# A hybrid decoder layer: the order of the state-space batches, and one run of value products for two attention units

## The chip, the cores and the metric

One core of one Trainium2 chip runs the whole layer (1024 tokens, width 1024, batch 1). The metric is the device time of one execution in microseconds.

## The reference, cut to what matters

The input is normed and projected once; half of the channels go through a diagonal complex state-space recurrence (32 groups of 16 channels, 64 states each), half through an attention over a window of 128 tokens with a sink; both are gated, joined by `w_out`, and a gated per-layer embedding follows.

```python
def s5_branch(u, lam_re, lam_im, log_step, b_re, b_im, c_re, c_im, d, w_glu, b_glu):
    lam_bar = jnp.exp(lam * step)
    b_bar = ((lam_bar - 1.0) / lam)[..., None] * b
    bu = jnp.einsum('blgp,gnp->blgn', uf.astype(jnp.complex64), b_bar)
    _, states = lax.associative_scan(combine, (a, bu), axis=1)
    y = jnp.einsum('blgn,gpn->blgp', states, c).real + d * uf
    g = jax.nn.gelu(y)
    return g * jax.nn.sigmoid(g @ w_glu + b_glu)

def swa_branch(q, k, v, sinks):        # 128 queries see the block before and their own
    scores = jnp.einsum('bnqkgd,bnskd->bnkgqs', qb, kb) * scale
    scores = jnp.where(mask, scores + bias, -jnp.inf)
    m = jnp.maximum(jnp.max(scores, axis=-1, keepdims=True), sink)
    e = jnp.exp(scores - m)
    probs = e / (jnp.sum(e, axis=-1, keepdims=True) + jnp.exp(sink - m))
    return jnp.einsum('bnkgqs,bnskd->bnqkgd', probs, vb)

proj = rms_norm(h, pre_norm_g) @ w_in           # u, z_ssm, q, k, v, z_attn
ssm_out  = s5_branch(u, ...) * silu(z_ssm)
attn_out = swa_branch(q, k, v, sinks) * silu(z_attn)
h = h + rms_norm(concat(ssm_out, attn_out) @ w_out, post_norm_g)
h = h + sigmoid(h @ pl_w_gate + pl_b_gate) * (p @ pl_w_proj)
```

## The kernel before

Most products run in two rounded parts of each operand (`split_to` makes a high and a low part, L91): for each slice of 128 of the contracted axis and each half of 512 tokens there are three matmuls, high by high (L122), high weight by low (L124), low weight by high (L126); `product` issues them. Weights come by DMA into `w_st` and are split by ScalarE (high part, L92) and VectorE (low part, L93).

A planner orders the instructions of every engine ahead of the run: it takes them by priority, which is the order of the program, and by its own model of time. `tc.high_priority(offset=AHEAD)` moves what stands in it 20 places forward; `tc.issue_after(i)` puts instructions behind `i` on the queue of `i`'s engine; `tc.manual_schedule(engines=...)` keeps the engine's instructions in the order of the program. Tiles with one tag share the buffers of `BUFS`; a tile waits until the one before it in its buffer is done with. The queues of all engines are fixed before the run; an instruction that waits holds up those behind it on its engine.

**State-space stage.** The 32 groups go in eight batches of four. For a batch, `into_states` loads the inputs `U` and the coefficients `coef` (SyncE queue), builds the input matrix `mt` (VectorE, three products, L530 to L532), transposes it on TensorE into a bank `tab` (L536) and copies it to `m` (ScalarE), multiplies it by `U` into `w` (L541, copied by ScalarE, L543), sends the halves of `w` crosswise into `w2` (`swapped`, DMAs issued by ScalarE, L591 and L592), makes the direct term (`t7`, through DRAM into `tz`) and the output matrix `qt` (three VectorE products). `phases` makes cosines `co` and sines `si` (six VectorE products). `scan` turns `w` by the phases, scans along time (four `tensor_tensor_scan`, L602) into `s` and swaps `s` into `s2` (DMAs on the SyncE queue). `outputs` turns `s` back, multiplies by `tz` and `qt` into a bank (L615, L617), applies the Gelu (L619) and stores `y` to DRAM. All VectorE products of these functions go through `tt`, so their line is L335. The order is `scan(b)`, `phases(b+1)`, `outputs(b)`, `into_states(b+1)`. `w` and `s` share the two buffers of tag `w`; `w2`, `s2` and `y` the two of tag `sw`; `tz`, `qt`, `co`, `si`, `U` and `coef` have two each, `mt` and `m` one. Between the batches stand the projections of v, q and the gates (11 tiles, 48 matmuls each).

**Attention.** Eight blocks of 128 queries, two units each (`half` 0 and 1, four heads each), so 16 units. A unit's steps: `scores` (TensorE, two banks `tab`, L764 and L765), `maxima` (VectorE, L773 and L781), `exponents` (ScalarE, L788), `normalized` (VectorE for half 0, L798, ScalarE for half 1, L796), `transposed` (TensorE into bank `w` or `y`, L803, copied to `p` by ScalarE, L805), `parted` (VectorE, L811), `values` (TensorE, L821, into the same bank: eight instructions, 64 weight columns each, on one half of the array's columns or the other by kv head; four in block 0), `gated` (VectorE, L826). Every other matmul of the stage uses all 128 columns. A unit starts every four ticks, and a step runs its lag later: `values` at 9 ticks, `gated` at 10. ScalarE's part of the attention stands behind the last batch's Gelu.

**Pieces.** Three ticks in four also run one piece of other TensorE work: 16 pieces of the last two SSM gate projections (`SsmGate`, six matmuls each), from piece 16 on the GLU products (`Glu`, L903, four instructions each), then the state-space half of the output product (`OutHalf`, six matmuls each). Pieces up to 9 stand ahead of the first unit. The GLU reads `y_all`, which is loaded from the stored `y`.

Of the kernel before, what the change touches and what calls it, by code (L numbers as in the profile page):

```python
# [20 lines left out]
P = 128  # L21
# [6 lines left out]
PC = 16  # L28
# [25 lines left out]
def layer_kernel(  # L54
# [6 lines left out]
    with ExitStack() as top:  # L61
# [272 lines left out]
        def tt(o, a, b, op):  # L334
            V.tensor_tensor(out=o, in0=a, in1=b, op=op)  # L335
# [144 lines left out]
        def big(name, tag):  # L480
            return t2([P, WID], F32, name, tag)
# [16 lines left out]
        def of_in(L, c):  # L498
            return L[:, c * GB : c * GB + GB, :].unsqueeze(2).broadcast_to([P, GB, PC, CH])
# [4 lines left out]
        def view_in(t):  # L504
            return t.rearrange("p (g q k) -> p g q k", k=CH, q=PC)
# [4 lines left out]
        def ev(t):  # L510
            return t.rearrange("p (g a b) -> p g a b", a=8, b=16)

        def into_states(b):

            c = b["c"]
            gs = slice(c * GB, (c + 1) * GB)
            U = b["U"] = t2([P, GB, NC], F32, "U", "u")
            nc.sync.dma_start(out=U, in_=u_dr[c // 2][(c % 2) * 64 : (c % 2) * 64 + 64].rearrange("(g q) j c -> (q j) g c", q=PC))
            coef = b["coef"] = t2([P, GB, 4, PC], F32, "coef", "coef")
            with tc.issue_after(loaded.ins):  # L520
                nc.sync.dma_start(out=coef, in_=bc[:, gs])

            t1, mt = big("t1", "ta"), big("mt", "mt")
            def per_in(n):
                return coef[:, :, n, :].unsqueeze(3).broadcast_to([P, GB, PC, CH])

            def per_out(n):
                return coef[:, :, n, :].unsqueeze(2).broadcast_to([P, GB, CH, PC])

            tt(view_in(t1), of_in(LB_re_, c), per_in(0), ALU.mult)  # L530
            tt(view_in(mt), of_in(LB_im_, c), per_in(1), ALU.mult)
            tt(mt, t1, mt, ALU.subtract)  # L532
            m = big("m", "m")
            ps = bank("tab")
            for g in range(GB):
                PE.transpose(ps[:, g * P : (g + 1) * P], mt[:, g * P : (g + 1) * P], ident)  # L536
            S.copy(out=m, in_=ps)
            w = b["w"] = big("w", "w")
            ps = bank("w")
            for g in range(GB):  # L540
                PE.matmul(ps[:, g * NC : (g + 1) * NC], lhsT=m[:, g * P : (g + 1) * P], rhs=U[:, g, :],  # L541
                          start=True, stop=True)
            S.copy(out=w, in_=ps)  # L543
            b["w2"] = swapped(w, nc.scalar)
            ps = bank("tab")
            for g in range(GB):
                PE.matmul(ps[:, g * PC : (g + 1) * PC], lhsT=mt[:, g * P : (g + 1) * P],
                          rhs=coef[:, g, 2, :], start=True, stop=True)
            t7 = b["t7"] = t2([P, GB, PC], F32, "t7", "t7")
            tt(t7, last.unsqueeze(1).broadcast_to([P, GB, PC]),  # L550
               ddt[:, gs].unsqueeze(2).broadcast_to([P, GB, PC]), ALU.mult)
            tt(t7, t7, ps[:, 0 : GB * PC].rearrange("p (g q) -> p g q", q=PC), ALU.add)


            n, o = 2 * CH * PC, t7_dr[c].offset
            tz = b["tz"] = big("tz", "tz")
            for g in range(GB):
                nc.sync.dma_start(out=bass.AP(tensor=t7_dr.tensor, offset=o + g * PC * n + n - PC, ap=[[n, PC], [-PC, CH], [1, PC]]), in_=t7[:, g, :])
            for g in range(GB):
                nc.sync.dma_start(out=tz[:, g * P : (g + 1) * P],  # L560
                                  in_=bass.AP(tensor=t7_dr.tensor, offset=o + g * PC * n + CH * PC, ap=[[n, PC], [-PC, CH], [1, P]]))
            a, qt = big("t2", "ta"), big("qt", "qt")
            tt(view_out(a), of_out(L_re, c), per_out(2), ALU.mult)
            tt(view_out(qt), of_out(L_im, c), per_out(3), ALU.mult)
            tt(qt, a, qt, ALU.add)
            b["qt"] = qt

        def phases(b):
            gs = slice(b["c"] * GB, (b["c"] + 1) * GB)
            co, si = b["co"], b["si"] = big("co", "co"), big("si", "si")  # L570

            def a_(t):
                return t[:, gs, :].unsqueeze(3).broadcast_to([P, GB, 8, 16])

            def b_(t):
                return t[:, gs, :].unsqueeze(2).broadcast_to([P, GB, 8, 16])

            a = big("t3", "ta")
            tt(ev(a), a_(e1[1]), b_(e0[1]), ALU.mult)
            tt(ev(co), a_(e1[0]), b_(e0[0]), ALU.mult)  # L580
            tt(co, co, a, ALU.subtract)
            a = big("t4", "ta")
            tt(ev(a), a_(e1[0]), b_(e0[1]), ALU.mult)
            tt(ev(si), a_(e1[1]), b_(e0[0]), ALU.mult)
            tt(si, si, a, ALU.add)

        swaps = []

# [5 lines left out]

        def scan(b):
            w, w2, co, si, c = (b[n] for n in ("w", "w2", "co", "si", "c"))
            tt(w2, w2, si, ALU.mult)
            tt(w, w, co, ALU.mult)
            tt(w, w, w2, ALU.add)
            s = b["s"] = big("s", "w")  # L600
            for g in range(GB):
                V.tensor_tensor_scan(out=s[:, g * NC : (g + 1) * NC],  # L602
                                     data0=r8[:, c * GB + g : c * GB + g + 1].broadcast_to([P, NC]),
                                     data1=w[:, g * NC : (g + 1) * NC], initial=0.0, op0=ALU.mult, op1=ALU.add)
            b["s2"] = swapped(s, nc.sync)

        def outputs(b):
            s, s2, co, si, c, U, tz, qt = (b[n] for n in ("s", "s2", "co", "si", "c", "U", "tz", "qt"))
            tt(s2, s2, si, ALU.mult)
            tt(s, s, co, ALU.mult)  # L610
            tt(s, s, s2, ALU.subtract)
            y = t2([P, GB, NC], F32, "y", "sw")
            ps = bank("y")
            for g in range(GB):
                PE.matmul(ps[:, g * NC : (g + 1) * NC], lhsT=tz[:, g * P : (g + 1) * P], rhs=U[:, g, :],  # L615
                          start=True, stop=False)
                PE.matmul(ps[:, g * NC + 1 : (g + 1) * NC], lhsT=qt[:, g * P : (g + 1) * P],  # L617
                          rhs=s[:, g * NC : (g + 1) * NC - 1], start=False, stop=True)
            b["gelu"] = S.activation(y, ps.rearrange("p (g c) -> p g c", c=NC), AF.Gelu_apprx_tanh)  # L619
            for g in range(GB):  # L620
                r = (c % 2) * 64 + g * PC
                b["stored"] = nc.sync.dma_start(out=y_dr[c // 2][r : r + PC].rearrange("q i c -> i q c"), in_=y[:, g, :])
# [62 lines left out]
        batch = [dict(c=c) for c in range(G // GB)]  # L685
        k_copies = [partial(copy_k, kv, part) for kv in range(2) for part in (kk_hi, kk_lo)]
        with tc.high_priority(offset=AHEAD):
            into_states(batch[0])
            phases(batch[0])
        project_k()  # L690
# [1 line left out]
                 + [partial(project_z_ssm, m) for m in range(2)])  # L692
        for c, b in enumerate(batch):
            with tc.high_priority(offset=AHEAD):
                scan(b)
                if c + 1 < len(batch):
                    phases(batch[c + 1])
                outputs(b)
                if c + 1 < len(batch):
                    into_states(batch[c + 1])  # L700
            for f in tiles[len(tiles) * c // len(batch) : len(tiles) * (c + 1) // len(batch)]:
                f()
                if k_copies and c > 1:
                    with tc.issue_after(w_last[0].ins):
                        k_copies.pop()()
# [260 lines left out]
        def run_pieces(lo, hi):  # L966
            for n in range(lo, hi):
                for f in pieces.get(n, ()):
# [1 line left out]

        units = [Unit(i) for i in range(2 * NB)]

        steps = ((Unit.gated, 10), (Unit.values, 9), (Unit.transposed, 6), (Unit.parted, 6), (Unit.normalized, 5),
                 (Unit.exponents, 3), (Unit.maxima, 1), (Unit.scores, 0))
        n, ahead, end = min(pieces), 10, max(pieces) + 1
        run_pieces(n, ahead)
        n = ahead
        bq = {0: queries(0)}
        for t in range(4 * len(units) + steps[0][1]):
            for step, lag in steps:  # L980
                i, r = divmod(t - lag, 4)
                if r == 0 and 0 <= i < len(units):
                    with tc.high_priority(offset=AHEAD), behind(ssm_end["gelu"]):
                        step(units[i])
            if t % 8 == 3 and t // 8 + 1 < NB:
                bq[t // 8 + 1] = queries(t // 8 + 1)
            if t % 4 != 1:
                run_pieces(n, n + 1)
                n += 1
        run_pieces(n, end)  # L990


        pls = []
# [191 lines left out]
```

## Time and profile before

| | us |
|---|---|
| median of 3 runs | 532.2 (531.94 to 533.16) |
| profiled execution, its own time | 531.67 |
| its span, first to last instruction | 529.9 |
| TensorE matmul busy | 516.9 (98%) |
| TensorE weight load busy | 409.0 (77%) |
| VectorE busy | 374.6 (71%) |
| ScalarE busy | 211.7 (40%) |

A row of a timeline gives the start, the time until the last of its instructions ended, engine, line, operation, names, shapes and count; in brackets the engine's idle time ahead of it and what ended that. A matmul's record is longer than the time after which the next one can end, since matmuls overlap: what one costs is read from end to end. A queue entry has the engine's name with a q behind it.

### The profile page before, as it was taken

The page shows a single profiled execution, that of the slowest core. Times are in us where ns is not written, and L with a number is a line of the kernel's source. Part 1 is how long each engine was busy: PE and PEld are TensorE (multiplying, and loading weights), DVE is VectorE, ACT ScalarE, POOL GpSimd, SP SyncE. Part 2 cuts the span into 40 slices and gives each one's busy share as a digit, 9 for nine tenths or more (in the row PEclk, how much of TensorE's full clock was granted, in tenths as well). Part 3 has the DMA queues.
Part 4 walks back from the last instruction along what each step waited for, and adds up shares of the span by engine and source line. Part 5 has one row for each costly group of instructions (what it writes and reads, how often), then busy time and mean ns, then how long its engine had stood idle before and what let it go on. Part 6 is the DMA issues. An engine that isn't in the chain of part 4 may idle for free.

```text
span 529.9 us, 7312 instructions
## 1 busy us (share of the span) xinstructions
PE 516.9 (98%) x2477; PEld 409.0 (77%) x2477; DVE 374.6 (71%) x865; ACT 211.7 (40%) x442; POOL 27.5 (5%) x69
## 2 busy tenths in 40 slices
PE   7999999999999999997899999999999999999996
PEld 6888888888888888884355766777788788888886
DVE  4879999879789979654878566555756659846232
ACT  5875121311222222124655655566734343333221
POOL 1000000000000000204020211100000000000000
PEclk9999999999999999999799999999999999999999
DMA  7972633445343344547755222101112155125112
GB/s 265 375 239 61 232 86 98 126 109 156 106 127 103 95 137 114 168 140 216 244 176 169 81 71 49 51 21 41 61 58 80 43 176 154 46 81 177 61 40 79
DMA packets 47092, 65.04 MB, mean 123 GB/s; under 512 B 10064, under 2 KB 25936, under 8 KB 47056
## 3 DMA queue, kind: packets, MB, share of 16 engines
q1 hardware_dynamic: 43664, 58.09, 34.5%
q0 software_dynamic: 1536, 4.20, 3.3%
q10 hardware_dynamic: 1856, 2.31, 1.7%
q8 instruction: 19, 0.31, 0.3%
q14 instruction: 17, 0.14, 0.1%
HBM read 44.12 MB, written 11.01 MB: 104 GB/s over the span
## 4 chain that ended last, share of the span: by engine, by line
PE 51%; DMA 2%; DVE 1%; SPq 0%; issue 0%; ACT 0%; ACTq 0%
PE ps_mm L126 9%; PE ps_mm L124 9%; PE ps_mm L122 9%; PE ps_mm L903 5%; PE ps_tab L122 3%; PE ps_tab L124 3%; PE ps_tab L126 3%; PE ps_w L821 2%; PE ps_y L821 2%; PE ps_tab L764 1%; PE ps_tab L765 1%; DMA y_all<-y_dr 1%; PE ps_w L803 1%; PE ps_y L803 1%; DMA y_dr<-y 1%
## 5 line engine op out<-in xcount | busy, mean ns | idle before, releaser
L122 PE MATMUL ps_mm<-x_hi,w_hi 128*128 128x512 f32 x272 | 86.2, 394 | 1.1 <-ACT x_hi L190 1.1
L126 PE MATMUL ps_mm<-x_hi,w_lo 128*128 128x512 f32 x272 | 86.9, 394 | 0.0
L124 PE MATMUL ps_mm<-x_lo,w_hi 128*128 128x512 f32 x272 | 85.7, 393 | 0.7 <-DVE x_lo L191 0.6
L92 ACT ACTIVATE w_hi<-w_st 128x512 fp32r<-128x512 f32 (+1 forms) x63 | 39.1, 621 | 100.9 <-PE ps_mm L124 68.9
L122 PEld LDWEIGHTS ps_mm<-x_hi,w_hi 128*128 128x128 f32 x272 | 50.9, 189 | 11.5 <-ACT x_hi L190 1.5
L124 PEld LDWEIGHTS ps_mm<-x_lo,w_hi 128*128 128x128 f32 x272 | 50.7, 188 | 11.6 <-DVE x_lo L191 1.5
L93 DVE TENSOR_TENSOR w_lo<-w_st,w_hi 128x512 fp32r<-128x512 f32 (+1 forms) x63 | 42.3, 671 | 24.3 <-ACT w_hi L92 24.3
L126 PEld LDWEIGHTS ps_mm<-x_hi,w_lo 128*128 128x128 f32 x272 | 50.7, 188 | 10.0
L903 PE MATMUL ps_mm<-y_all,w_glu 128*128 128x512 f32 x64 | 31.4, 637 | 3.5 <-DMA y_all<-y_dr 3.4
L122 PE MATMUL ps_mm<-h_hi,w_hi 128*128 128x512 f32 (+1 forms) x96 | 30.8, 380 | 0.0
L124 PE MATMUL ps_mm<-h_lo,w_hi 128*128 128x512 f32 (+1 forms) x96 | 30.8, 380 | 0.0
L126 PE MATMUL ps_mm<-h_hi,w_lo 128*128 128x512 f32 (+1 forms) x96 | 30.7, 380 | 0.0
L788 ACT ACTIVATE sc<-sc,mx 128x129 f32<-128x129 f32 x64 | 25.1, 395 | 12.7 <-DVE mx L781 12.5
L903 PEld LDWEIGHTS ps_mm<-y_all,w_glu 128*128 128x128 f32 x64 | 12.3, 203 | 17.7 <-issue 12.5
L1082 DVE SCALAR_TENSOR_TENSOR o_t<-o_t,pls 128x512 f32<-128x512 f32 (+1 forms) x17 | 10.8, 657 | 19.7 <-ACT o_t L1081 19.7
L335 DVE TENSOR_TENSOR sw<-sw,si 128x512 f32<-128x512 f32 x16 | 11.0, 686 | 16.5 <-DMA sw<-s 9.0
L122 PE MATMUL ps_mm<-m_hi,w_hi 128*128 128x512 f32 x64 | 22.1, 405 | 0.0
L126 PE MATMUL ps_mm<-m_hi,w_lo 128*128 128x512 f32 x64 | 21.8, 398 | 0.0
L124 PE MATMUL ps_mm<-m_lo,w_hi 128*128 128x512 f32 x64 | 21.7, 403 | 0.0
L122 PEld LDWEIGHTS ps_mm<-h_hi,w_hi 128*128 128x128 f32 x96 | 18.0, 188 | 3.5
L124 PEld LDWEIGHTS ps_mm<-h_lo,w_hi 128*128 128x128 f32 x96 | 18.1, 188 | 3.5
L126 PEld LDWEIGHTS ps_mm<-h_hi,w_lo 128*128 128x128 f32 x96 | 18.0, 188 | 3.4
(281 smaller groups left out, 1036.7 us busy)
## 6 DMA issues: line engine op xcount, KB each, us to landing
w_st<-in_w_in SPq DMA_DIRECT2D x30, 256.0 KB
w_st<-in_w_out SPq DMA_DIRECT2D x16, 256.0 KB
w_st<-in_w_gate SPq DMA_DIRECT2D x16, 256.0 KB
x<-in_xS SPq DMA_DIRECT2D x8, 512.0 KB
out_T<-o_t SPq DMA_DIRECT2D x15, 256.0 KB
x_sq<-in_xT SPq DMA_DIRECT2D x4, 512.0 KB
x_st<-in_x SPq DMA_DIRECT2D x4, 512.0 KB
x_sq<-in_x SPq DMA_DIRECT2D x4, 512.0 KB
```

What stands on the lines that cost most here:

```text
L92: S.activation(hi, t, AF.Copy)
L93: V.tensor_tensor(out=lo, in0=t, in1=hi.bitcast(F32), op=ALU.subtract)
L122: yield PE.matmul(o, lhsT=wh, rhs=ah(ka, h), start=f, stop=False)
L124: yield PE.matmul(o, lhsT=wh, rhs=al(ka, h), start=False, stop=False)
L126: yield PE.matmul(o, lhsT=wl, rhs=ah(ka, h), start=False, stop=l)
L335: V.tensor_tensor(out=o, in0=a, in1=b, op=op)
L764: PE.matmul(o, lhsT=l, rhs=kk_hi[:, kv, k0 : k0 + wk], start=True, stop=False)
L788: S.activation(self.sc[:, m, :], self.sc[:, m, :], AF.Exp, bias=self.mx[:, m : m + 1], scale=-1.0, accum_out=self.sm[:, m : m + 1])
L803: PE.transpose(pt[:, m * P : (m + 1) * P], self.sc[:, m, 0:P], ident)
L821: PE.matmul(pv[64 * kv : 64 * kv + 64], lhsT=v[:, cols], rhs=p[:, 2 * kv : 2 * kv + 2, :], start=n == 0, stop=n == len(parts) - 1)
L903: PE.matmul(self.ps, lhsT=self.w[:, k, :], rhs=glu_in["y"][:, self.hf, k, :], start=k == 0, stop=k == 3)
L1082: V.scalar_tensor_tensor(out=t, in0=t, scalar=1.0, in1=pls[2 * m + h][:, a : a + n], op0=ALU.add, op1=ALU.mult)
```

## The change

Three parts. The first is the order of the state-space batches: the first half of `into_states` becomes a function `inputs` (loads, `mt`, its transposition, `m`), and the order becomes `inputs(b+1)`, `scan(b)`, `into_states(b+1)`, `phases(b+1)`, `outputs(b)`, with the three VectorE products of `outputs(b)` (two of them explicitly) queued behind the last products of `into_states(b+1)` (`made`) and `phases(b+1)` (`turned`). No buffer is added. The second: `values` runs 12 ticks after the start of a unit of half 0 and 8 after one of half 1, `gated` at 13 and 9, so both units of a block multiply on the same tick. The third: TensorE goes in program order from the first piece to the last.

```diff
-        def into_states(b):
+        def inputs(b):
...
             t1, mt = big("t1", "ta"), big("mt", "mt")
+            b["mt"] = mt
...
             S.copy(out=m, in_=ps)
+
+        def into_states(b):
+
+            c, U, coef, m, mt = (b[n] for n in ("c", "U", "coef", "m", "mt"))
...
-            tt(qt, a, qt, ALU.add)
+            b["made"] = V.tensor_tensor(out=qt, in0=a, in1=qt, op=ALU.add)
...
-            tt(si, si, a, ALU.add)
+            b["turned"] = V.tensor_tensor(out=si, in0=si, in1=a, op=ALU.add)
...
         def scan(b):
             w, w2, co, si, c = (b[n] for n in ("w", "w2", "co", "si", "c"))
+            tt(w, w, co, ALU.mult)
             tt(w2, w2, si, ALU.mult)
-            tt(w, w, co, ALU.mult)
...
-        def outputs(b):
+        def outputs(b, behind):
             s, s2, co, si, c, U, tz, qt = (b[n] for n in ("s", "s2", "co", "si", "c", "U", "tz", "qt"))
-            tt(s2, s2, si, ALU.mult)
-            tt(s, s, co, ALU.mult)
+
+            with ExitStack() as after:
+                for i in behind:
+                    after.enter_context(tc.issue_after(i.ins))
+                tt(s, s, co, ALU.mult)
+                tt(s2, s2, si, ALU.mult)
             tt(s, s, s2, ALU.subtract)
...
         for c, b in enumerate(batch):
             with tc.high_priority(offset=AHEAD):
+                following = batch[c + 1] if c + 1 < len(batch) else None
+                if following:
+                    inputs(following)
                 scan(b)
-                if c + 1 < len(batch):
-                    phases(batch[c + 1])
-                outputs(b)
-                if c + 1 < len(batch):
-                    into_states(batch[c + 1])
+                if following:
+                    into_states(following)
+                    phases(following)
+                outputs(b, [following["made"], following["turned"]] if following else [])
...
-        steps = ((Unit.gated, 10), (Unit.values, 9), (Unit.transposed, 6), (Unit.parted, 6), (Unit.normalized, 5),
-                 (Unit.exponents, 3), (Unit.maxima, 1), (Unit.scores, 0))
+        steps = ((Unit.gated, 13, 9), (Unit.values, 12, 8), (Unit.transposed, 6, 6), (Unit.parted, 6, 6), (Unit.normalized, 5, 5),
+                 (Unit.exponents, 3, 3), (Unit.maxima, 1, 1), (Unit.scores, 0, 0))
...
+        with tc.manual_schedule(engines={mybir.EngineType.PE}):
+            run_pieces(n, ahead)
+            n = ahead
+            bq = {0: queries(0)}
+            for t in range(4 * len(units) + steps[0][2]):
+                for step, half, i in [(s, h, (t - lags[h]) // 4) for s, *lags in steps for h in range(2) if (t - lags[h]) % 4 == 0]:
+                    if 0 <= i < len(units) and i % 2 == half:
+                        with tc.high_priority(offset=AHEAD), behind(ssm_end["gelu"]):
+                            step(units[i])
+                if t % 8 == 3 and t // 8 + 1 < NB:
+                    bq[t // 8 + 1] = queries(t // 8 + 1)
+                if t % 4 != 1:
+                    run_pieces(n, n + 1)
+                    n += 1
+            run_pieces(n, end)
```

## Rows read from the trace of the kernel before

**Rows 1.** The profile page, its first part: busy time, share of the span and instructions of each engine.

```profile
PE 516.9 (98%) x2477; PEld 409.0 (77%) x2477; DVE 374.6 (71%) x865; ACT 211.7 (40%) x442; POOL 27.5 (5%) x69
```

**Rows 2.** Busy time by stretch: the stretch and its length, busy time and instructions of PE, PEld, DVE, ACT and POOL, then TensorE's granted clock (1.00 is 2.4 GHz), share of the DMA engines, GB/s.

```profile
105.00:238.50 133.50, 133.50 (x703) 114.19 (x701) 108.87 (x195) 29.35 (x44) 4.56 (x8) 1.00 0.45 126
238.50:252.00 13.50, 10.15 (x45) 5.98 (x43) 6.36 (x17) 5.86 (x16) 6.17 (x12) 1.00 0.80 216
252.00:259.00 7.00, 5.47 (x10) 2.78 (x11) 4.96 (x17) 3.12 (x6) 0.70 (x1) 0.51 0.86 283
...
271.00:380.00 109.00, 109.00 (x533) 74.45 (x532) 72.00 (x236) 68.73 (x204) 13.14 (x30) 1.00 0.26 74
```

**Rows 3.** Timeline of TensorE where the state-space stage ends: the last matmuls of `SsmGate`, GLU products (L903), the last batch's output products, scores, the first unit's transposes and the first value products (L821).

```profile
238.04 0.62 PE L124 MATMUL ps_mm<-x_lo,w_hi 128*128 128x512 f32 x2
238.50 0.61 PE L126 MATMUL ps_mm<-x_hi,w_lo 128*128 128x512 f32 x2
240.14 1.96 PE L903 MATMUL ps_mm<-y_all,w_glu 128*128 128x512 f32 x4 [1.03 <-DMA y_all<-y_dr]
...
243.49 3.95 PE L903 MATMUL ps_mm<-y_all,w_glu 128*128 128x512 f32 x8
...
250.37 0.38 PE L764 MATMUL ps_tab<-kk,bq 128*128 128x256 f32 x1 [1.33 <-ACT sc L767]
...
253.53 3.78 PE L903 MATMUL ps_mm<-y_all,w_glu 128*128 128x512 f32 x4 [2.42 <-DMA y_all<-y_dr]
257.11 1.06 PE L803 MATMUL ps_w<-ident,sc 128*128 128x128 f32 x4
257.96 4.07 PE L903 MATMUL ps_mm<-y_all,w_glu 128*128 128x512 f32 x8
261.95 0.65 PE L821 MATMUL ps_w<-p,v_f 128*64 128x256 f32 x4
262.54 7.13 PE L903 MATMUL ps_mm<-y_all,w_glu 128*128 128x512 f32 x16
```

**Rows 4.** Timeline of TensorE in the attention: value products of one unit taken in pieces of two instructions between scores, those of another unit in one stretch, and the last stretch of the kernel.

```profile
281.06 0.28 PE L765 MATMUL ps_tab<-kk,bq 128*128 128x256 f32 x1
281.27 0.65 PE L821 MATMUL ps_w<-p,v_f 128*64 128x256 f32 x2
281.85 0.38 PE L764 MATMUL ps_tab<-kk,bq 128*128 128x256 f32 x1
...
304.34 0.61 PE L122 MATMUL ps_mm<-m_hi,w_hi 128*128 128x512 f32 x2
304.88 0.65 PE L821 MATMUL ps_w<-p,v_f 128*64 128x256 f32 x4
305.37 0.60 PE L821 MATMUL ps_w<-p_own,v_step 128*64 128x256 f32 x4
305.90 0.50 PE L124 MATMUL ps_mm<-m_lo,w_hi 128*128 128x512 f32 x1
...
376.10 0.65 PE L821 MATMUL ps_y<-p,v_f 128*64 128x256 f32 x4
```

**Rows 5.** The end of the state-space stage: two of VectorE's waits between 105 and 242 us (in total, times, longest), then rows of ScalarE's and VectorE's timelines.

```profile
DVE sw L335 <- DMA sw<-s: 9.0, 4, 3.1
...
DVE sw L335 <- DMA t_dr<-t: 5.6, 2, 3.0
...
217.31 0.56 ACT L543 COPY w<-ps_w 128x512 f32<-128x512 f32 x1
225.47 0.63 ACT L92 ACTIVATE bq_hi<-q_f 128x512 fp32r<-128x512 f32 x1 [7.60 <-PE ps_y L615]
225.98 0.47 ACTq L591 DMA_DIRECT2D sw<-w  x1
...
244.01 0.58 ACT L619 ACTIVATE y<-ps_y 128x512 f32<-128x512 f32 x1
...
230.81 0.69 DVE L335 TENSOR_TENSOR sw<-sw,si 128x512 f32<-128x512 f32 x1 [1.93 <-DMA sw<-w]
...
234.48 1.37 DVE L602 TENSOR_TENSOR_SCAN s<-r,w 128x128 f32<-128x128 f32 x4
238.96 0.69 DVE L335 TENSOR_TENSOR sw<-sw,si 128x512 f32<-128x512 f32 x1 [3.12 <-DMA sw<-s]
...
253.51 0.87 DVE L798 TENSOR_SCALAR sc<-sc,sm 128x128 f32<-128x128 f32 x4
```

**Rows 6.** Groups of instructions between 265 and 380 us by line, VectorE's and ScalarE's: busy time of the group, mean ns of one, idle time of the engine just before them and what ended it.

```profile
L781 DVE CUSTOM_DVE_ANT_0 sc<-ps_tab,bias,sink 128x128 f32<-128x128 f32 x52 | 15.7, 347 | 0.9 <-DVE ps_tab L773 0.2
L773 DVE COPY_PREDICATED ps_tab<-own,ps_tab 128x256 f32<-128x256 int32 x26 | 11.0, 425 | 6.8 <-PE ps_tab L765 6.5
L93 DVE TENSOR_TENSOR w_lo<-w_st,w_hi 128x512 fp32r<-128x512 f32 x12 | 8.2, 683 | 2.0 <-ACT w_hi L92 2.0
L798 DVE TENSOR_SCALAR sc<-sc,sm 128x128 f32<-128x128 f32 x28 | 6.2, 282 | 0.2
...
L788 ACT ACTIVATE sc<-sc,mx 128x129 f32<-128x129 f32 x52 | 20.4, 395 | 12.7 <-DVE mx L781 12.5
L788 ACT ACTIVATION_READ_ACCUMULATOR sc<-sc,mx 128x1 f32 x52 | 9.8, 189 | 0.0
L796 ACT ACTIVATE sc<-sc,sm 128x128 f32<-128x128 f32 x28 | 9.1, 393 | 1.4 <-DVE sm L793 1.4
```

More of the change, by code (lines that the diff above doesn't have):

```diff
@@ L511, in ev, with per_in, per_out @@
             return t.rearrange("p (g a b) -> p g a b", a=8, b=16)
-        def into_states(b):
+        def per_in(b, n):
+            return b["coef"][:, :, n, :].unsqueeze(3).broadcast_to([P, GB, PC, CH])
+        def per_out(b, n):
+            return b["coef"][:, :, n, :].unsqueeze(2).broadcast_to([P, GB, CH, PC])
+        def inputs(b):
             c = b["c"]
@@ L523, in into_states @@
             t1, mt = big("t1", "ta"), big("mt", "mt")
[L524 to L531, printed above, removed]
+            b["mt"] = mt
+            tt(view_in(t1), of_in(LB_re_, c), per_in(b, 0), ALU.mult)
+            tt(view_in(mt), of_in(LB_im_, c), per_in(b, 1), ALU.mult)
             tt(mt, t1, mt, ALU.subtract)
-            m = big("m", "m")
+            m = b["m"] = big("m", "m")
             ps = bank("tab")
@@ L537, in into_states @@
             S.copy(out=m, in_=ps)
+        def into_states(b):
+            c, U, coef, m, mt = (b[n] for n in ("c", "U", "coef", "m", "mt"))
+            gs = slice(c * GB, (c + 1) * GB)
             w = b["w"] = big("w", "w")
@@ L562, in into_states @@
             a, qt = big("t2", "ta"), big("qt", "qt")
-            tt(view_out(a), of_out(L_re, c), per_out(2), ALU.mult)
-            tt(view_out(qt), of_out(L_im, c), per_out(3), ALU.mult)
-            tt(qt, a, qt, ALU.add)
+            tt(view_out(a), of_out(L_re, c), per_out(b, 2), ALU.mult)
+            tt(view_out(qt), of_out(L_im, c), per_out(b, 3), ALU.mult)
+            b["made"] = V.tensor_tensor(out=qt, in0=a, in1=qt, op=ALU.add)
             b["qt"] = qt
@@ L687, in layer_kernel @@
         with tc.high_priority(offset=AHEAD):
+            inputs(batch[0])
             into_states(batch[0])
@@ L971, in layer_kernel @@
         units = [Unit(i) for i in range(2 * NB)]
-        steps = ((Unit.gated, 10), (Unit.values, 9), (Unit.transposed, 6), (Unit.parted, 6), (Unit.normalized, 5),
-                 (Unit.exponents, 3), (Unit.maxima, 1), (Unit.scores, 0))
+        steps = ((Unit.gated, 13, 9), (Unit.values, 12, 8), (Unit.transposed, 6, 6), (Unit.parted, 6, 6), (Unit.normalized, 5, 5),
+                 (Unit.exponents, 3, 3), (Unit.maxima, 1, 1), (Unit.scores, 0, 0))
         n, ahead, end = min(pieces), 10, max(pieces) + 1
[L976 to L990, printed above, removed]
+        with tc.manual_schedule(engines={mybir.EngineType.PE}):
[13 more added lines that the diff above has]
+            run_pieces(n, end)
         pls = []
```

## Prediction

> **What bounds the kernel now.** The page comes first: TensorE is busy 98% of the span, no other engine over 77% [rows 1]. So only two things can shorten the run: TensorE's few empty or slow stretches, and matmuls that cost more than their columns. The table by stretch shows where to look [rows 2]. From 105 to 238.5 us and from 271 to 380 us TensorE is never empty at the full clock. Between lies one bad place: busy 10.15 of 13.5 us, and then 7 us at a mean granted clock of 0.51, nearly all of it the lower level, 1.2 GHz. The timeline of that place says why [rows 3]: the last gate projection ends at 239.11, the GLU waits for `y_all`, scores wait for ScalarE, the GLU waits again. The slow clock begins after this half-empty stretch. The last batch's Gelu starts only at 244.01 [rows 5]. Here the end of the state-space chain ends last, and TensorE has run out of other work.
>
> The second reading is of the value products inside the full stage [rows 4]. Two 512-column instructions end 0.453 us apart in pairs (238.04 + 0.62 to 238.50 + 0.61, about 0.23 each) [rows 3]; two score instructions about 0.12 each. Around L821 this breaks. The score before ends at 281.34, the two value instructions at 281.92, the next score at 282.23: 0.58, and 0.31 in place of 0.12. So a stretch of L821 costs an entry, and about 0.19 after it on whatever follows. A whole unit in one stretch ends at 305.97 after 304.95: 1.02 for eight, and the next matmul takes 0.43 for 0.23.
>
> **Part one: value products.** From the first stretch [rows 3] to the last [rows 4] the timeline has 31 stretches of L821: 17 of two instructions, 6 of four, one of six, 7 of eight, 120 in all. A stretch of four costs what one of two costs: 262.03 to 262.60 is 0.57 [rows 3]. So the two halves of the columns work side by side, and pieces of two waste that as well. Now: 23 x 0.58 + 1.01 + 7 x 1.02 = 21.5 us, and 31 x 0.19 = 5.9 us behind them, 27.4 us. After: block 0 is one stretch of eight (1.02), seven blocks one of sixteen each. Four more instructions cost 1.02 - 0.58 = 0.44, so sixteen cost 1.02 + 0.88 = 1.90. 7 x 1.90 + 1.02 + 8 x 0.20 = 15.9 us. That is 11.5 us less, on the engine that is never empty there, so all of it counts. It needs both units of a block to be contiguous on TensorE: on one tick the list of steps gives `values` of half 0, then of half 1, and program order lets nothing between.
>
> The Trainium skill (TensorEngine Tiling (Array Packing), Key Properties) says only that a change of tiling mode drains TensorE. By that rule alone the saving would be 23 fewer changes at 0.15 + 0.19, 7.8 us, and the sum below would come to 521.6. The stretches of two and four, which cost the same, speak for the larger number.
>
> **Part two: the end of the state-space stage.** From 239.11 to 262.03 pass 22.9 us. Work done in it at the full rate: 24 GLU instructions at 0.43 (16 in 6.9 us, 262.54 onward, less the 0.2 at its start) 10.3; 16 scores, 16 output products of the last batch and 4 transposes, all taken at the scores' 0.12, 4.3; in all 14.6 us [rows 3, 4]. Lost: 8.3 us, of it some 2 by the clock. With the 11.5 this is the most that the change can give: 531.7 - 11.5 - 8.3 = 511.9 us.
>
> How much comes back depends on when the last Gelu ends (244.6 now) and what TensorE can do meanwhile. Why is it late? `w` of the last batch is copied at 217.87, but its swap is issued at 225.98: it stands on ScalarE's queue behind a `bq_hi` that waits 7.60 us for batch 6's outputs [rows 5]. In the new order `w2` takes the buffer that `scan(6)` frees, not one that `outputs(6)` frees, so the planner can put the swap right behind the copy. That makes the last scan 8 us earlier (Gelu at 236.6). Then VectorE's waits for swaps, 9.0 and 5.6 us [rows 5], 11.5 of it ahead of the last batch. In the new order `into_states(b+1)` and `phases(b+1)` stand between a scan and the use of its swap: nine products of 0.6 us, longer than the swap's 3. I take half of these waits as gained, 6 us, since VectorE also serves the projections, whose work does not move: Gelu at about 230.5. Bounds: 244.6 (nothing gained) and 225 (all of it). The swap's DMAs keep their queues; `U` and `coef` are asked for a batch half earlier on SyncE, behind nothing that waits longer than now. The price: `outputs(b)` comes later on VectorE, and `scan(b+1)` needs `s`'s buffer (tag `w`) back from it; with chain pieces of about 12 us in a batch that takes 20 us now, this is covered.
>
> Program order takes something back here. Now all 16 gate pieces run before the attention; after, pieces 13 to 15 stand behind `scores` of the second unit, which need the banks that ScalarE empties after the Gelu. So TensorE runs dry at 239.1 - 3 x 1.36 = 235.0, and after the Gelu it has 0.9 us of scores and 1.36 us of piece 13 before `transposed` of the first unit. That comes 9.8 us after the Gelu's end (244.59 to 254.38, when the first unit is normalized) [rows 5]. The empty time is Gelu + 9.8 - 237.3, here 3.0 us; 0 at 225, 9.1 at 236.6, 17.1 at 244.6. For the clock I add 0.5 us: a quarter of the 2 that it cost after a longer hole.
>
> **Part three: program order in the attention.** It adds waits: an instruction whose input is late now holds everything behind it, pieces included, which would need no input of the attention. Two distances matter. Between the scores of a half-1 unit and its transposes stand four pieces (5.4), four transposes (0.44) and one set of scores (0.94): 6.8 us; for half 0 also the value run, 8.9 us. The chain that must fit [rows 6]: two L773 0.85, four L781 about 1.2 (started 0.27 apart), four exponents 1.6 + 0.19, and normalizing, on ScalarE 1.6, on VectorE 1.1: 5.4 and 4.9 us, a reciprocal and the handovers not counted. The margin is under 1.4 us for half 1, under 4.0 for half 0. VectorE is busy 72.0 and ScalarE 68.7 of 109 us there [rows 2], so one alien instruction ahead (0.68, L93) fits, two don't. I take 0.25 us for each of eight half-1 units, 2 us. Bounds: 0 (the trace of now has no wait in 109 us), and 3 us for each block, 24 us, if the queues of VectorE and ScalarE put the chain last. `values` of half 1 a tick earlier than now has two pieces (2.7 us) for a copy and a `parted`; that fits. Half 0's longer hold of bank `w` meets `transposed` of the next block only after 0.86 + 0.94 + 1.36 us, in which VectorE must do `gated`, two products of half the columns of L93's 0.68: nothing.
>
> **Sum.** 511.9 + 3.0 + 0.5 + 2.0 = 517.4 us against the profiled execution's own 531.67. The median of the runs lies 0.5 above that one, so the forecast is 517.9 us.
>
> **The rivals.** (a) *The batches end only as early as the freed swap makes them*, the Gelu at 236.6: empty time 9.1 in place of 3.0, and the full 2 us of clock: 511.9 + 9.1 + 2 + 2 + 0.5 = 525.5. Speaks for it: VectorE's queue is 82% busy up to 238.5 [rows 2], so reordering may only move its waits. (b) *The overlap isn't got at all*, since no buffer is added: `s` and `w`, and `w2`, `s2` and `y`, still share two. The Gelu stays at 244.6, and program order, which withholds three pieces, leaves 17.1 us empty: 511.9 + 17.1 + 2 + 2 + 0.5 = 533.5, the gain of part one eaten. Against it: the order of tags lets `w(b+1)` and `w2(b+1)` in right after `scan(b)`. The Trainium skill (Perfetto Trace Analysis, Optimization Strategy) reads gaps that repeat as too few buffers for the next tile; by that rule the waits for `sw` would stay, which is this case. (c) *TensorE waits in the attention*, the one that ends slower: the place is L803 of half 1, the price what its chain exceeds 6.8 us by. Without its 2 us the forecast is 515.9, so from (532.2 - 515.9) / 8 = 2.0 us for each block it decides; at 3 us the time is 539.9. (d) *The value products aren't one run*, because the planner still lets others between: without part one, 529.4.
>
> **Chances.** Forecast 0.62, (a) 0.17, (b) 0.08, (c) 0.10, (d) 0.03. Between 511.5 (511.9 + 0.5, less 0.9 for reading errors) and 527 lie the forecast, (a) and part of (c) with small waits; (b), (d) and the dear half of (c) are left out. A change of 0.2% (1.1 us) is about what a measurement of this kernel can tell from none. Faster: forecast, (a), (d), a third of (b) and 0.03 of (c), 0.88; same: half of (b), 0.04; slower: the rest, 0.08.
>
> **What would show it.** Eight stretches of L821 and some 16 us for them shows part one; more stretches refute it. The last L619 before 235 us, no wait of VectorE for `sw<-s`, and the swap of the last `w` within 1 us of its copy show part two; an L903 or L803 behind an empty TensorE shows how much is left, and a row at clock 0.5 what it cost. Waits of TensorE at L803 after 271 us, twice in each block, would show (c). The prediction is wrong above all if the planner, which orders VectorE and ScalarE by its own model of time, puts `outputs` or the attention's chain late.

## The result and the profile after

The changed kernel takes 522.75 us (522.39 to 523.7) against 532.07 us beside it: a ratio of 0.9826, 95% interval 0.9804 to 0.9849. Forecast were 517.9 us, range 511.5 to 527. The profiled execution's span is 520.7 us, 9.2 us shorter. In what follows runs from different chips are compared by their ratio to the kernel before on the same chip; times "at 532.1" are that ratio times 532.1 us. A hole is a stretch in which TensorE is empty.

TensorE by stretch (columns as in [rows 2]), of the kernel after:

```profile
105.00:230.00 125.00, 125.00 (x661) 106.90 (x660) 107.59 (x198) 30.30 (x46) 6.18 (x14) 1.00 0.50 135
230.00:245.00 15.00, 14.75 (x75) 11.62 (x74) 7.26 (x26) 7.77 (x24) 3.54 (x7) 1.00 0.70 210
245.00:262.00 17.00, 13.79 (x48) 7.14 (x49) 11.18 (x37) 10.79 (x33) 2.44 (x6) 0.90 0.68 212
262.00:370.00 108.00, 104.94 (x536) 75.86 (x535) 72.49 (x230) 66.37 (x195) 10.61 (x25) 0.98 0.26 76
```

The bad place of [rows 2] has shrunk, but the attention, never empty before, now has 3 us empty and a clock below 1.00. The waits of TensorE (in total, times, longest) and the ends of the empty stretches say where:

```profile
PE ps_y L816 <- ACT sc L809: 6.5, 2, 3.5
```

```profile
242.76 0.28 PE L778 MATMUL ps_tab<-kk,bq 128*128 128x256 f32 x1
242.87 1.88 PE L916 MATMUL ps_mm<-y_all,w_glu 128*128 128x512 f32 x4
248.21 1.26 PE L816 MATMUL ps_y<-ident,sc 128*128 128x128 f32 x4 [3.46 <-ACT sc L809]
249.26 4.79 PE L916 MATMUL ps_mm<-y_all,w_glu 128*128 128x512 f32 x8
...
290.35 0.62 PE L126 MATMUL ps_mm<-m_hi,w_lo 128*128 128x512 f32 x2
294.03 1.20 PE L816 MATMUL ps_y<-ident,sc 128*128 128x128 f32 x4 [3.06 <-ACT sc L809]
294.99 0.71 PE L122 MATMUL ps_mm<-m_hi,w_hi 128*128 128x512 f32 x2
295.54 0.62 PE L124 MATMUL ps_mm<-m_lo,w_hi 128*128 128x512 f32 x2
296.00 1.01 PE L126 MATMUL ps_mm<-m_hi,w_lo 128*128 128x512 f32 x2
296.81 1.05 PE L122 MATMUL ps_mm<-m_hi,w_hi 128*128 128x512 f32 x2
297.67 1.05 PE L124 MATMUL ps_mm<-m_lo,w_hi 128*128 128x512 f32 x2
298.52 1.05 PE L126 MATMUL ps_mm<-m_hi,w_lo 128*128 128x512 f32 x2
```

Two holes, both ahead of the transposes (L816 now) of a half-1 unit, whose normalizing (L809) is ScalarE's. What stands behind them is GLU products at the first and output products at the second, which needed nothing of the attention. Behind each hole stands a stretch at the lower clock (columns as in [rows 2]):

```profile
248.25:251.65 3.40, 3.40 (x7) 1.73 (x8) 1.50 (x6) 2.70 (x12) 0.19 (x1) 0.50 0.81 305
294.03:296.03 2.00, 2.00 (x9) 1.36 (x10) 1.13 (x7) 1.40 (x4) 0.19 (x1) 1.00 0.29 99
296.05:299.44 3.39, 3.39 (x9) 2.22 (x7) 0.53 (x1) 0.00 (x0) 0.00 (x0) 0.50 0.05 18
```

Behind the first hole it comes at once. Behind the second it comes after 2 us of work: matmul pairs first end 0.45 us apart, then 0.86 (297.86 to 298.72 and 299.57). At half the clock 3.4 us lose 1.7, so by the rows the holes with their clock cost 3.46 + 3.06 + 1.7 + 1.7 = 9.9 us.

The value products (L834 now), one of the seven long stretches, answer to [rows 4]:

```profile
267.31 1.02 PE L916 MATMUL ps_mm<-y_all,w_glu 128*128 128x512 f32 x2
268.26 0.65 PE L834 MATMUL ps_w<-p,v_f 128*64 128x256 f32 x4
268.74 0.60 PE L834 MATMUL ps_w<-p_own,v_step 128*64 128x256 f32 x4
269.18 0.60 PE L834 MATMUL ps_y<-p,v_f 128*64 128x256 f32 x4
269.61 0.60 PE L834 MATMUL ps_y<-p_own,v_step 128*64 128x256 f32 x4
270.14 0.39 PE L777 MATMUL ps_tab<-kk,bq 128*128 128x256 f32 x1
```

From 268.33 to 270.21, 1.88 us for sixteen, and 0.32 for the next score in place of 0.12. There are eight stretches: 7 x 1.88 + 1.02 + 8 x 0.20 = 15.8 us, against 27.4: 11.6 us less. The whole change is then 532.1 - 8.3 (the loss at the state-space end) - 11.6 + 9.9 = 522.1 us, for 522.75 measured: what the value products gave, the two holes took again but for some 2 us.

The state-space end, ScalarE's timeline at the swap of the last batch, and the Gelu's group (shortest, middle and longest ns, first and last start), against [rows 5]:

```profile
188.46 0.59 ACT L549 COPY w<-ps_w 128x512 f32<-128x512 f32 x1 [2.08 <-PE ps_w L547]
189.07 0.48 ACTq L597 DMA_DIRECT2D sw<-w  x1
```

```profile
L629 ACT ACTIVATE y<-ps_y x8: 581/598/598, 102.9 to 211.9; 128x512 f32<-128x512 f32 x8
```

The swap is issued as its copy ends, and the last Gelu starts at 211.9, not 244.0. Between the start of the first scan and the end of the last Gelu VectorE (the third engine in the row) looks like this, before and then after:

```profile
89.90:244.60 154.70, 153.59 (x811) 130.03 (x809) 125.21 (x225) 35.78 (x55) 6.16 (x13) 1.00 0.46 130
```

```profile
89.90:212.50 122.60, 122.60 (x672) 105.56 (x671) 115.59 (x217) 32.39 (x51) 5.34 (x13) 1.00 0.50 134
```

VectorE's idle time fell from 29.5 to 7.0 us, and 9.6 us of its work, most of it the gates' (`z_half`, `z_tanh`, `w_lo`), now comes after the Gelu: 22.5 + 9.6 = 32.1 us, the whole of the Gelu's shift. The waits for `sw<-s` are not quite gone; the longest that is left is the last batch's, which no batch follows:

```profile
DVE s L335 <- DMA sw<-s: 3.1, 2, 2.6
```

### The profile page after: what moved, and what is told of

Same layout as the page of the kernel before. It is cut to its first block, busy times and chain, and to the rows that moved or that the text cites. A ratio compares the mean times of both kernels' runs of the same rounds, so it can differ in the third digit from the quotient of the medians.

```text
span 520.7 us, 7280 instructions
## 1 busy us (share of the span) xinstructions
PE 506.0 (97%) x2477; PEld 407.7 (78%) x2477; DVE 371.7 (71%) x865; ACT 211.0 (41%) x442; POOL 24.8 (5%) x69
## 4 chain that ended last, share of the span: by engine, by line
PE 92%; DMA 3%; DVE 2%; SPq 1%; ACT 1%; issue 0%; DVEq 0%
PE ps_mm L122 21%; PE ps_mm L126 21%; PE ps_mm L124 21%; PE ps_mm L916 5%; PE ps_tab L122 4%; PE ps_tab L124 4%; PE ps_tab L126 4%; PE ps_w L834 1%; DMA z_th<-z_dr 1%; PE ps_tab L777 1%; PE ps_y L627 1%; PE ps_y L625 1%; PE ps_w L547 1%; PE ps_y L834 1%; PE ps_tab L778 1%; DMA x_st<-in_xT 1%
## 5 line engine op out<-in xcount | busy, mean ns | idle before, releaser
L122 PE MATMUL ps_mm<-x_hi,w_hi 128*128 128x512 f32 x272 | 88.1, 397 | 1.0 <-ACT x_hi L190 1.0
L93 DVE TENSOR_TENSOR w_lo<-w_st,w_hi 128x512 fp32r<-128x512 f32 (+1 forms) x63 | 42.3, 672 | 33.9 <-ACT w_hi L92 30.0
L126 PE MATMUL ps_mm<-m_hi,w_lo 128*128 128x512 f32 x64 | 20.7, 405 | 0.0
L916 PEld LDWEIGHTS ps_mm<-y_all,w_glu 128*128 128x128 f32 x64 | 11.9, 200 | 10.8 <-issue 10.8
L124 PE MATMUL ps_mm<-m_lo,w_hi 128*128 128x512 f32 x64 | 20.3, 399 | 0.0
L1096 ACT ACTIVATE o_t<-ps_mm,hb_gate 128x512 f32<-128x512 f32 (+1 forms) x12 | 7.7, 665 | 24.8 <-PE ps_mm L126 15.9
```

Of the source, the lines that this page charges most:

```text
L93: V.tensor_tensor(out=lo, in0=t, in1=hi.bitcast(F32), op=ALU.subtract)
L122: yield PE.matmul(o, lhsT=wh, rhs=ah(ka, h), start=f, stop=False)
L124: yield PE.matmul(o, lhsT=wh, rhs=al(ka, h), start=False, stop=False)
L126: yield PE.matmul(o, lhsT=wl, rhs=ah(ka, h), start=False, stop=l)
L916: PE.matmul(self.ps, lhsT=self.w[:, k, :], rhs=glu_in["y"][:, self.hf, k, :], start=k == 0, stop=k == 3)
L1096: S.activation(t, o, AF.Tanh, bias=hb_gate[:, m : m + 1], scale=0.5)
```

## The experiments

Each is an edit of the changed kernel unless it says otherwise.

| run | us | ratio, 95% interval | at 532.1 |
|---|---|---|---|
| whole change | 522.75 | 0.9826 (0.9804 to 0.9849) | 522.8 |
| e1 batches alone | 523.89 | 0.9854 (0.9823 to 0.9885) | 524.3 |
| e2 attention alone | 535.2 | 1.0065 (1.0036 to 1.0095) | 535.6 |
| e3 old lags | 517.62 | 0.9737 (0.9700 to 0.9773) | 518.1 |
| e4 no program order | 519.42 | 0.9769 (0.9742 to 0.9795) | 519.8 |
| e5 not behind `made`, `turned` | 522.57 | 0.9799 (0.9735 to 0.9864) | 521.4 |
| e6 values at 13 and 9 | 520.63 | 0.9745 (0.9701 to 0.9788) | 518.5 |
| e7 16 pieces ahead | 519.78 | 0.9723 (0.9678 to 0.9768) | 517.4 |
| e8 e6 and e7 | 514.11 | 0.9629 (0.9586 to 0.9673) | 512.4 |
| e9 no empty pieces | 517.04 | 0.9729 (0.9715 to 0.9742) | 517.7 |
| e10 only `inputs` early | 535.11 | 1.0064 (1.0041 to 1.0088) | 535.5 |
| e11 e8 and e9 | 512.66 | 0.9641 (0.9628 to 0.9654) | 513.0 |

**e1, e2: the two halves apart.** The new batches with the old attention loop, and the old batches with the new one.

> The new order of the state-space batches alone, the attention as before (31 stretches of value products, no program order). First theory (each part pays for itself, and program order in the attention makes two holes of its own): the Gelu of the last batch near 212 us, the loss of 8.3 us at the end of the state-space stage gone, the values as dear as before: 532.1 - 8.3 = about 524 us. Rival (the state-space order is all of the gain, and part one is eaten by program order): the same time as with the whole change, 522.7 us, or less. What tells them apart more is the sum of this run's gain and that of the attention alone.

> The new lags and program order alone, the batches in the old order. First theory: 11.5 us saved on values, and the Gelu stays near 244 us, so that the hole at the end of the state-space stage grows from 8.3 to 17 us or more, as the prediction's rival (b) has it, and the later hole stays: between 530 and 536 us. Rival (program order gives nothing, the batches all): no saving on values to be seen either, 535 us or more with more than eight stretches of values.

The batches alone give 7.8 us: the hole at the end of their stage is gone (TensorE busy 32.00 of 32 us from 230 to 262), and 31 stretches of values remain. The attention alone loses 3.5 us. It has eight stretches, so the saving is there, but TensorE waits 6.0 us for the last batch's outputs, whose Gelu starts at 244.1 us as before:

```profile
PE ps_y L617 <- DVE s L335: 6.0, 1, 6.0
PE ps_y L803 <- ACT sc L796: 3.8, 2, 3.1
PE ps_w L803 <- DVE sc L798: 2.3, 1, 2.3
```

For e2 the first theory holds. For e1 the time doesn't decide: 524.3 us (522.7 to 526.0) is what the first theory expected, and can't be told from the 522.8 of the whole change, which its rival expected. Both are right in part: the batches give 7.8 of the 9.3 us, and the attention's own saving goes into its holes. The two gains alone sum to 7.8 - 3.5 = 4.3 us, not 9.3, so the parts aren't independent: program order with the new lags costs more than it gives unless the Gelu comes early.

**e3, e4: one run of two units, and program order, each taken back.**

```diff
-        steps = ((Unit.gated, 13, 9), (Unit.values, 12, 8),
+        steps = ((Unit.gated, 10, 10), (Unit.values, 9, 9),
```

> The whole change but with values at 9 ticks and gated at 10 for both units, so each unit multiplies values by itself: 16 stretches. First theory: eight stretches more at 0.15 + 0.19 us each, 2.7 us, with the same two holes at the transposes: 525.4 us. Rival (the run of two units itself makes the holes, as it moves what stands between scores and transposes): the holes go and the time is below 521 us.

```diff
-        with tc.manual_schedule(engines={mybir.EngineType.PE}):
+        with ExitStack():
             run_pieces(n, ahead)
```

> The whole change without program order on TensorE in the attention. The planner then makes 22 stretches of values: 5 of two instructions, 4 of four, 2 of six, 11 of eight, 18.4 us and 22 x 0.19 us behind them, 22.5 us against 15.7 us. First theory (the two holes at the transposes and the slow clock behind them, some 11 us, are the price of program order): 522.7 + 6.8 - 11 = 518.5 us. Rival (the holes come from late inputs whatever the order of TensorE): they stay, 529.5 us.

Both are faster than the whole change, by 4.7 and 3.0 us at 532.1. For e3 the rival was right of the second hole: 16 stretches cost more, yet in its place there is only a wait of 0.7 us ahead of values, and the clock stays at 1.00 from 262 us on. The first hole stays, at 2.5 us. The old lags leave two units' values, each by itself, inside the window of a half-1 unit (between its scores and its transposes): they fall one tick and five ticks after the scores. The new ones take all of them out. For e4 the first theory was right: 22 stretches and no wait of TensorE in the attention, 519.8 for 518.5 expected. e4 and e1 differ in the lags alone: 22 stretches for 31 are 4.5 us less, where the prediction's 27.4 us for 31 and the 22.5 above for 22 let 4.9 be expected.

**e6, e7, e8: each hole by its own edit.**

```diff
# e6
+        steps = ((Unit.gated, 14, 10), (Unit.values, 13, 9),
# e7
+        n, ahead, end = min(pieces), 16, max(pieces) + 1
```

> The whole change with the run of values one tick later (13 and 9, gated 14 and 10): still eight stretches, but the run now stands between the scores of a half-1 unit and its transposes, 8.7 us in place of 6.8 us. First theory (the second hole, 3.1 us and the slow clock behind it, comes from the narrow window of half 1, since the run was taken out of it): that hole goes, 522.7 - 5 = 517.5 us. Rival (it comes from the two pieces without TensorE work between GLU and output product): the hole stays, 521 us or more.

> The whole change with all sixteen gate pieces ahead of the attention (16 for 10). First theory (the first hole, 3.5 us, its single transposes and the slow clock, comes from the last gate's z_half, which stands on VectorE ahead of the second unit's maxima and waits for pieces 14 and 15): it goes, 522.7 - 5 = 517.5 us. Rival (the first block's chain with its table load is too long for any order): the hole moves to another of the first transposes, 521 us or more.

> Values at 13 and 9 and all gate pieces ahead: both holes gone by the first theory, 512.5 us, near the floor of 511.9 + 0.5 us that the prediction worked out. By the rivals of the two runs beside it, 519 us or more.

4.3, 5.4 and 10.4 us less than the whole change at 532.1, so the two holes with their clock are worth some 10 us and, within intervals of some 2.5 us each, add up; the first theory was right in all three. In e6 TensorE waits 1.4 us for bank `w` instead, which the later values hold longer. (In all three runs the last block's two units fell apart: nine stretches of values, not eight.) With both edits TensorE's stretches, to be read against the first table of this part:

```profile
230.00:245.00 15.00, 15.00 (x63) 10.77 (x61) 5.81 (x13) 5.62 (x13) 0.64 (x1) 1.00 0.74 248
245.00:262.00 17.00, 17.00 (x65) 8.94 (x66) 15.11 (x52) 12.46 (x42) 6.11 (x11) 1.00 0.68 213
262.00:370.00 108.00, 107.47 (x575) 80.79 (x572) 73.60 (x233) 69.66 (x204) 11.04 (x26) 1.00 0.25 77
```

For the first hole VectorE's and ScalarE's rows of the changed kernel show the way in, and e7, in which the gate's pieces stand ahead, has no first hole:

```profile
241.88 1.09 DVE L879 SCALAR_TENSOR_TENSOR z_half<-ps_mm,preb 128x512 f32<-128x512 f32 x1 [4.96 <-PE ps_mm L126]
242.81 0.32 DVE L794 CUSTOM_DVE_ANT_0 sc<-sc,bias,sink 128x128 f32<-128x128 f32 x1
...
243.18 0.41 ACT L801 ACTIVATE sc<-sc,mx 128x129 f32<-128x129 f32 x1 [3.24 <-DVE mx L794]
244.96 1.06 ACT L886 ACTIVATE z_tanh<-z_half 128x1024 f32<-128x1024 f32 x1
247.14 0.63 ACT L92 ACTIVATE bq_hi<-q_f 128x512 fp32r<-128x512 f32 x1 [1.12 <-DMA bq<-bq_hi]
247.68 1.26 ACT L809 ACTIVATE sc<-sc,sm 128x128 f32<-128x128 f32 x4
...
245.49 0.17 DVE L806 RECIPROCAL sm<-sm 128x4 f32<-128x4 f32 x1
```

The second unit's maxima stand on VectorE behind the last gate's `z_half`, which waits 4.96 us for the pieces that program order put behind the first units. Then its normalizing, whose reciprocal is there at 245.66, stands on ScalarE behind that gate's tanh and a `bq_hi` until 247.68. Which of these instructions alone would make the hole was not tried.

The second hole has a late chain of its own besides the narrow window:

```profile
286.20 0.28 PE L778 MATMUL ps_tab<-kk,bq 128*128 128x256 f32 x1
...
290.92 0.19 ACT L801 ACTIVATION_READ_ACCUMULATOR sc<-sc,mx 128x1 f32 x1
...
293.31 0.17 DVE L806 RECIPROCAL sm<-sm 128x4 f32<-128x4 f32 x1
...
293.59 1.26 ACT L809 ACTIVATE sc<-sc,sm 128x128 f32<-128x128 f32 x4
```

The unit's scores end at 286.48, its sums are there at 291.11, its reciprocal comes only at 293.31, behind the next unit's maxima and products of other work on VectorE, and the transposes start at 294.03. The chain took 7.55 us; the work in its window was done at 290.97, after 4.5 us.

**e9, e11: the empty pieces.** Between GLU and output product two pieces hold no TensorE work.

```diff
-        n += 2
         for m in range(KT):
             OutHalf(m, n)
```

> The whole change (values at 12 and 8) without the two pieces between GLU and output product that hold no TensorE work: the output product's pieces start two earlier. First theory, sharpened by the run with values at 13 (the second hole needs both: the window of half 1, 6.8 us without the values, and two empty pieces in it, which leave 4.1 us): with all pieces full the hole is gone, 517.5 us. Rival (the empty pieces only mark the place, the window is too narrow anyway): the hole moves to another block, 521 us or more.

> Values at 13 and 9, all gate pieces ahead, no empty pieces. First theory: no hole is left to remove, only single transposes that wait for ScalarE's heads one by one, so 513.5 to 514.5 us, the same as without the last edit. Rival (the empty pieces still cost where the first output pieces wait): below 513 us.

e9 removes the second hole too, with the narrow window left as it is; TensorE's one wait at L816 is the first hole's, 3.7 us. So e3 and e6 had not yet told the two conditions apart: the hole needs the narrow window and two empty pieces in it. e11 is no better than e8 (0.9641 in 0.9628 to 0.9654, against 0.9629 in 0.9586 to 0.9673), as the first theory had it, though 513.0 at 532.1 lies under its range and on its rival's bound.

**e5, e10: what moved the Gelu.**

```diff
# e5
-                outputs(b, [following["made"], following["turned"]] if following else [])
+                outputs(b, [])
# e10
+                inputs(following); scan(b); phases(following); outputs(b, []); into_states(following)
```

> The whole change without putting the products of outputs(b) behind made and turned: the order of the functions stays. First theory (VectorE, no longer idle on swaps, is what moved the last Gelu from 244 to 212 us, and the explicit order does that): waits of VectorE for swaps come back in part, the Gelu lands between 220 and 235 us; as TensorE has other work until 235 us the time changes by less than 2 us if the Gelu stays before 228 us, and by up to 8 us beyond. Rival (the order of the functions and the freed buffer do it alone): Gelu at 212 us and 522.7 us.

> The whole change, but of the batches only inputs(b+1) stays early: then scan(b), phases(b+1), outputs(b), into_states(b+1), as before the change. First theory (what moved the last Gelu is that the rest of into_states and phases stand between a scan and the use of its swap, and that w2 gets the buffer that the scan frees): the Gelu falls back to 235 to 244 us, TensorE is empty there as in the run of the attention alone, 530 to 535 us. Rival (loading and transposing the inputs a half batch earlier is what did it): the Gelu stays below 220 us, 522.7 us.

e5 changes nothing: the rival was right, TensorE, VectorE and ScalarE run the same instructions in the same order as with the whole change, and the last Gelu starts at 211.9 again. The 1.4 us between 521.4 and 522.8 are thus what two measurements of one order can differ by, and the lower clock behind the first hole lasts 6.8 us here, not 3.4:

```profile
246.95:253.78 6.83, 6.28 (x11) 2.94 (x12) 3.38 (x9) 3.99 (x15) 0.19 (x1) 0.50 0.69 235
```

e10 puts the last Gelu back to 243.1 and loses the whole gain, so the first theory was right. `phases` stands between a scan and the use of its swap in e10 too, as before the change; what counts is that the rest of `into_states` stands ahead of `outputs`. Without it VectorE waits 11.9 us for `sw<-s`, and the last swap is issued at 224.12, 11.4 us behind its copy. How much of the shift is VectorE's filling and how much the earlier swap was not tried apart.

## Why the prediction was right and where it was not

**Part one, right in count and size.** Eight stretches, 15.8 us for 15.9; e8 at the floor, below, shows that the saving counts in full once the holes are gone. By the rule of the Trainium skill alone (TensorEngine Tiling (Array Packing), Key Properties) the prediction's estimate was 7.8 us less; the rows after have 11.6 (27.4 - 15.8), so the larger reading holds. What the run of two units adds to the time beyond whole units isn't shown: e9 with eight stretches and e3 with sixteen, both without the second hole, differ by 0.4 us at 532.1, within their intervals, where 2.7 us were expected; their first holes differ too, 3.7 and 2.5 us.

**Part two, right in mechanism, wrong in size.** The swap went out behind its copy, as forecast. "I take half of these waits as gained, 6 us, since VectorE also serves the projections, whose work does not move" is the step that failed: it does move. It counted 14.6 us of waits where VectorE's idle time in the chain was 29.5; of that 22.5 us went, with no buffer added, and 9.6 us of other work besides, so the Gelu ended at 212.5 us, outside the bounds of 225 to 244.6. Its "nine products" between a scan and the use of its swap counted the six of `phases`, which stood there before in program order. In e1 the loss at the state-space end is gone (7.8 us gained of 8.3). In the whole change the 3.0 us that the formula adds for a Gelu at 230.5 were not gained, since a hole of another cause stood there.

**The empty time at the start, wrong in cause.** The formula (Gelu + 9.8 - 237.3) gives none for this Gelu, yet 3.46 us stood empty. It counted only the first unit's chain behind the Gelu. The second unit's chain stood behind the last gate's `z_half`, which program order had made late. The prediction named the three pieces held back, but not what waits for them on VectorE. That its 3.5 us came near the 5.2 of this hole and its clock is luck.

**Part three, the term that was mis-sized.** Forecast were 3.5 us for the start and 2 us, a quarter of a us in each of eight blocks. Found were two holes, worth 10.4 us together with their clock (whole change against e8; 9.9 by the rows). That is 4.9 us more than the 5.5 forecast, the whole distance between forecast and result. Rival (c) had the place and the mechanism, transposes of half 1 behind too narrow a window; the price wasn't paid in every block, but once, where two pieces were empty. Two figures failed there. The count "four pieces (5.4)" was two, so the window was 4.5 us for 6.8. The chain of 5.4 us took 7.55, as other work stood ahead on both queues, which the prediction had named as the danger ("one alien instruction ahead (0.68, L93) fits, two don't"). By its own 5.4 us the hole would have been 0.9 us, not 3.06. The 0.5 us for the clock was too small as well: 1.7 behind each hole. The floor of 511.9 + 0.5 us was right: e8 comes to 512.4 at 532.1 (510.1 to 514.7).

**Rival (b)** was about right as a price: 533.5 forecast, 535.6 in e2, where the Gelu stays at 244. Its terms were not: TensorE stood empty there for 10.1 us (6.0, 1.0, 2.3 and 0.7) and not 17.1, and 13.6 us at the lower clock and the later hole of 3.1 us made up for it.

## What to carry to other kernels

Program order on the busiest engine turns each late input into a hole for all that stands behind it; walk each chain's window tick by tick, with the pieces that are empty and with the instructions of other work that stand ahead on the slower engines' queues. Gather products of another array shape into one run, but look which window they were filling. A chain that waits for a DMA between two steps of one engine gained here, with the same buffers, from the next item's independent work put between these steps in program order.

## What the runs showed of the hardware

Two matmul instructions on the two halves of the array's columns take the time of one: a stretch of four costs 0.57 us and a stretch of two 0.58 [rows 3, 4]. Changing to that shape costs about 0.15 us on the way in (0.58 for the first four, 0.44 for four more) and 0.19 to 0.20 us on the score or the 512-column matmul that follows (0.31 for 0.12, 0.43 for 0.23).

With every hole of 2.5 us (e3) to 3.7 us (e9) came a stretch at TensorE's lower clock, 1.2 GHz; it began between 0.8 us before the end of the hole (e2) and 2 us after it (the second hole above). What that costs is not fixed: 3.4 us of it, so 1.7 us lost, for each hole of the whole change, but 6.8 us for a hole of 2.7 us in e5, whose order of instructions is the same. No such stretch came with waits of 0.4 to 0.95 us (e3, e6, e8).
